# The second set of triangular inverses queued on DVE behind step 12 of the first set

## The chip, the core and the metric

The kernel runs on one core of a Trainium2 chip. The metric is the time of one execution in microseconds on the device. The core's engines each work through their own queue in order: TensorE (PE), VectorE (DVE), ScalarE (ACT) and GpSimd (POOL). SyncE (SP) issues most of the DMA transfers; ACT issues some. An instruction starts when it is at the head of its engine's queue and the semaphores it needs are set.

## The reference

One layer of a diffusion backbone: 2048 latent and 256 context tokens of width 1024 are normalised and modulated, one projection feeds two mixers (a gated DeltaNet in both directions and windowed attention), and gates, two projections and an output projection follow. Cut to the branch that matters here:

```python
qa, ka, va, g, bt = _gdn_inputs(qkv, beta_r, decay_r, conv_w, a_log, dt_bias)
oa, _, _ = _gdn_bidir(qa, ka, va, g, bt, s_f, s_b, True)
ya = _gdn_output(oa, za, gdn_norm_w)               # za: a gate, silu
...
# inside _gdn_chunked, for each chunk of 64 tokens and each head
a_mat = jnp.where(strict, jnp.einsum('nbhik,nbhjk->nbhij', kb, kc) * decay, 0.0)
t_mat = lax.linalg.triangular_solve(a_mat, eye, left_side=True, lower=True, unit_diagonal=True)
u = jnp.einsum('nbhij,nbhjv->nbhiv', t_mat, vc * bc[..., None])
```

Each chunk of 64 tokens needs the inverse of a unit lower triangular 64x64 matrix, for four heads and two directions.

## The kernel before, in words

The kernel is one program for one core. It computes in float32, with each operand of a large matmul split into a high and a low part, so that a product takes three matmuls per slice of 128 rows. A scheduler sets the order of the instructions in each engine's queue at build time, from priorities (the order in which the code is written) and its own estimate of time. `tc.issue_after(x)` adds one rule: the instructions written inside the block come after `x` in the queue of the engine on which `x` runs. It adds no wait on the chip, and it says nothing of the other engines' queues.

The stages that matter, in the order of the code:

- **Convolutions** (`qkv`, `conv`, `finish`) of q, k and v. `last_conv[0]` is the DVE instruction (L565) that ends the last one.
- **Gate products for token groups 2 and 3** (`gates`, `rest`, `rest_run`, `fm_dense`). For each of 24 column tiles (m) `rest` loads a weight tile: L241 loads `wr` on SP, ACT rounds it to `wh` (L243), DVE takes the rest as `wl` (L246). For each token group `rest_run` runs 24 matmuls (8 slices, L524 to L526) into one of three PSUM buffers `rps`. ACT takes the tanh into one of two buffers `rt` (L816). For m below 8 DVE multiplies it with the product (L818) and so is the last reader of the PSUM buffer, and SP stores the result (L819). For m from 8 on ACT's tanh is the last reader, and ACT issues the store.
- **The modulation gate** (`mod_gate`) beside them, in two halves: SP loads eight `wmg` tiles (L220), ACT scales them (L221; the first of a half goes to `gacc`), POOL adds them up (L223), and PE sums over the partitions (L227).
- **The inverses** (`base`), twice: set 0 (context chunks and the chunks that the scan meets first) and set 1 (the chunks in the middle). A set holds 128 matrices of 64x64, one per partition, in a tile `N`; set 0's lies in the pool `bs` and set 1's in `bs2`. SP loads `nb` (L733) and `N` (L734), 2 MB for a set. DVE scales `N` in four slices of rows for each direction, eight instructions (L737 and L739), and then runs 62 steps of elimination: step m multiplies a column with a row into `btmp` (L747) and adds this to the rows below m (L749), over (63 - m) x m elements per partition, so that a step grows from 62 to 992 elements and shrinks again. POOL clears the upper triangle (L754) and SP stores the set (L759).
- **The scan** (`scan`, `chain`, `merge`, `output`) over 18 chunks in both directions, with gate products for token groups 1 and 0 as filling work for PE, and a last small set of inverses (`base4`). The scan's `v` is L1102.
- Attention, the projections and the output projection follow; the change doesn't touch them.

Both sets are written behind the gate products, each inside `tc.issue_after(last_conv[0].ins)`, so that DVE may start them as soon as the convolutions are over; the scheduler mixes their steps with the drains (L818) and the `wl` (L246) of the gate products.

Of the kernel before, what the change touches and what calls it, by code (L numbers as in the profile page):

```python
# [11 lines left out]
ALU = mybir.AluOpType  # L12
# [20 lines left out]
def hybrid(tc, ins, out, dbg=None, upto=9):  # L33
    nc = tc.nc
    V, S, G, T = nc.vector, nc.scalar, nc.gpsimd, nc.tensor
    ctx = ExitStack()
    with ctx:
        _hybrid(ctx, tc, nc, V, S, G, T, ins, out, dbg, upto)


def _hybrid(ctx, tc, nc, V, S, G, T, ins, out, dbg, upto):
# [514 lines left out]
    last_conv = [None]  # L556
# [153 lines left out]
    def runs(chunks):  # L710

        out = []
        for i, c in enumerate(chunks):
            if out and c == out[-1][1] + out[-1][2]:
                out[-1][2] += 1
            else:
                out.append([i, c, 1])
        return out

    def base(si, npool, pool, fr, bk):  # L720


        n = 8 * len(fr)
        h1 = max(32, n)
        N = npool.tile([128, 64, 64], F32, name="N")
        nb = npool.tile([128, 64], F32, name="nb")
        if n < h1:
            G.memset(N[0:h1], 0.0)
            G.memset(nb[0:h1], 0.0)
        for d, chunks in ((0, fr), (1, bk)):  # L730
            for i0, c, k in runs(chunks):
                p0 = d * h1 + i0 * 8
                dma(nb[p0:p0 + 8 * k], brT[c:c + k, d * 4:d * 4 + 4].rearrange("c h (b t) -> c (h b) t", b=2))  # L733
                dma(N[p0:p0 + 8 * k], Nsp[d][c:c + k].rearrange("c h b r i -> (c h b) r i"))  # L734
        for q in range(4):
            r, w = slice(q * 16, q * 16 + 16), q * 16 + 16
            V.tensor_tensor(N[0:h1, r, 0:w], N[0:h1, r, 0:w],  # L737
                            nb[0:h1, 0:w].unsqueeze(1).to_broadcast([h1, 16, w]), op=ALU.mult)
            V.tensor_tensor(N[h1:h1 + n, r, 0:w], N[h1:h1 + n, r, 0:w],  # L739
                            nb[h1:h1 + n, r].unsqueeze(2).to_broadcast([n, 16, w]), op=ALU.mult)  # L740
        yield 9
        A = N[0:h1 + n]
        for m in range(1, 63):
            tmp = pool.tile([128, 1376], F32, name="btmp")
            r = 63 - m
            tv = tmp[0:h1 + n, :r * m].rearrange("p (r j) -> p r j", j=m)
            V.tensor_tensor(tv, A[:, m + 1:, m].unsqueeze(2).to_broadcast([h1 + n, r, m]),  # L747
                            A[:, m, 0:m].unsqueeze(1).to_broadcast([h1 + n, r, m]), op=ALU.mult)
            V.tensor_tensor(A[:, m + 1:, 0:m], A[:, m + 1:, 0:m], tv, op=ALU.add)  # L749
            yield 2 * (65 + 1.04 * r * m) / 1e3  # L750

        for q in range(4):
            r, w = slice(q * 16, q * 16 + 16), 64 - q * 16
            G.affine_select(A[:, r, q * 16:], A[:, r, q * 16:], pattern=[[1, 16], [-1, w]], base=0,  # L754
                            channel_multiplier=0, compare_op=ALU.is_gt, fill=0.0)
        V.memset(A.rearrange("p r c -> p (r c)")[:, ::65], 1.0)
        for d, chunks in ((0, fr), (1, bk)):
            p0 = d * h1
            dma(Xset[d][si].rearrange("c h b r j -> (c h b) (r j)"), N[p0:p0 + n].rearrange("p r j -> p (r j)"))  # L759
            for ci, c in enumerate(chunks):  # L760
                Xsp[d][c] = Xset[d][si][ci]
        yield 1
# [82 lines left out]
    LAST = (LAT(14, 15), LAT(0, 1))  # L845
    for si, (fr, bk, np_) in enumerate((([0, 1] + LAT(*range(0, 6)), [0, 1] + LAT(*range(10, 16)), bs),
                                        (LAT(*range(6, 14)), LAT(*range(2, 10)), bs2))):
        with tc.issue_after(last_conv[0].ins):
            for _ in base(si, np_, bs2, fr, bk):
                pass  # L850
    last_base = base4(*LAST)
# [425 lines left out]
    with tc.tile_pool(name="p4h", bufs=1, side="right", reuse_waits="tile") as hr, \  # L1277
# [15 lines left out]
        A, Y = {}, {}  # L1293
# [265 lines left out]
```

## Time and profile before

| | |
|---|---|
| time, median of 3 runs | 2011.6 us (2008.56 to 2013.08) |
| the profiled execution's own time | 2014.61 us |
| its span, first to last instruction | 2012.8 us |
| granted TensorE clock, mean | 0.983 |
| L747, 124 instructions of both sets | 659.2 to 965.3 us, 114.6 us busy |
| L749, the same | 659.5 to 966.5 us, 118.5 us busy |
| L737 and L739, scalings of both sets | 645.7 to 674.5 us |
| MATMUL L524 to L526 into `rps` | 768 each, 309.7, 309.0 and 307.8 us busy |

Times in the text are microseconds from the span's start. In a time line a row gives start, length, engine, line, operation, tiles written and read, partitions x elements, and how many instructions are merged in it; the brackets at its end give how long the engine stood before it and whose end it waited for. A matmul's length in a row holds its passage through the array, so the rate of PE is read from starts. Lines have the numbers of the kernel before, unless it is said otherwise; in the kernel after, everything from `base` on stands two lines further down (L747 is L749 there, L749 is L751, L737 is L739, L739 is L741, L818 is L820, L1102 is L1104).

### The profile page before, as it was taken

To read this page: it belongs to the slowest core of one execution; us is meant where nothing else is said; L and a number is where in the kernel's file an instruction comes from. 1 tells how busy PE (TensorE), PEld (TensorE's weight loads), DVE (VectorE), ACT (ScalarE), POOL (GpSimd) and SP (SyncE) were. 2 spreads that over 40 slices of the span, in tenths; PEclk is the share of its full clock that TensorE was granted. 3 is DMA by queue.
4 is the path that set the end of the run, shared out by engine and by line. 5 is a ranking of instruction groups with operands and counts; after the bars stand their busy time and mean duration, and the time that the engine had idled before them with its cause. 6 is when DMAs were issued, how large, how long until landed. Compare 5 with 4: busy or idle time off the path is not lost. (4 is left out here: it accounts for less than half of the span.)

```text
span 2012.8 us, 32096 instructions
## 1 busy us (share of the span) xinstructions
PE 1924.7 (96%) x10947; PEld 1611.6 (80%) x10947; DVE 1501.4 (75%) x2871; ACT 807.2 (40%) x1998; POOL 689.5 (34%) x768
## 2 busy tenths in 40 slices
PE   6999999989999999999999999999989999998998
PEld 3888888779998778877888888888778888876776
DVE  6979766667776899999777776536687768756867
ACT  5755545544443322211222233225665646532211
POOL 1652111225543211004222234323555444410675
PEclk8999999999999999999999999999999999999999
DMA  7552326764546633537887777664455545364453
GB/s 258 168 136 84 102 88 157 191 159 148 161 147 162 183 112 111 140 100 221 225 241 220 237 207 211 185 208 152 144 173 176 187 149 180 106 206 146 152 157 131
DMA packets 387703, 333.12 MB, mean 165 GB/s; under 512 B 83992, under 2 KB 307536, under 8 KB 386900
## 3 DMA queue, kind: packets, MB, share of 16 engines
q1 hardware_dynamic: 352244, 288.60, 49.7%
q10 hardware_dynamic: 35296, 42.48, 6.0%
q8 instruction: 87, 1.43, 0.3%
q14 instruction: 76, 0.62, 0.1%
HBM read 220.28 MB, written 109.13 MB: 164 GB/s over the span
## 5 line engine op out<-in xcount | busy, mean ns | idle before, releaser
L524 PE MATMUL rps<-hh,wh 128*128 128x512 f32 x768 | 309.7, 403 | 5.2 <-DVE rt L818 4.1
L526 PE MATMUL rps<-hh,wl 128*128 128x512 f32 x768 | 309.0, 403 | 0.0
L525 PE MATMUL rps<-hl,wh 128*128 128x512 f32 x768 | 307.8, 401 | 0.0
L563 DVE SCALAR_TENSOR_TENSOR cacc<-y,cw,cacc 128x512 f32<-128x512 f32 (+1 forms) x224 | 162.1, 745 | 22.6 <-ACT cacc L561 18.2
L524 PEld LDWEIGHTS rps<-hh,wh 128*128 128x128 f32 x768 | 145.7, 190 | 40.1 <-DVE rt L818 4.5
L525 PEld LDWEIGHTS rps<-hl,wh 128*128 128x128 f32 x768 | 145.9, 190 | 32.9
L524 PE MATMUL lps<-hh,wh 128*128 128x512 f32 (+1 forms) x448 | 171.4, 383 | 0.3 <-ACT y L634 0.3
L526 PEld LDWEIGHTS rps<-hh,wl 128*128 128x128 f32 x768 | 145.6, 190 | 32.5
L526 PE MATMUL lps<-hh,wl 128*128 128x512 f32 (+1 forms) x448 | 171.3, 382 | 0.0
L525 PE MATMUL lps<-hl,wh 128*128 128x512 f32 (+1 forms) x448 | 171.3, 382 | 0.0
L945 DVE TENSOR_TENSOR pl<-pt,ph 128x512 fp32r<-128x512 f32 x156 | 105.3, 685 | 42.2 <-ACT ph L943 41.6
L943 ACT CAST ph<-pt 128x512 fp32r<-128x512 f32 x156 | 90.3, 585 | 112.6 <-PE pt L941 78.0
L917 DVE CUSTOM_DVE_ANT_0 pr<-sc,band,sk 128x640 f32<-128x640 f32 (+1 forms) x128 | 106.5, 861 | 33.5 <-PE sc L913 17.5
L816 ACT ACTIVATE rt<-rps 128x512 f32<-128x512 f32 x96 | 57.2, 596 | 182.0 <-PE rps L526 168.1
L749 DVE TENSOR_TENSOR N<-N,btmp 128x62 f32<-128x62 f32 (+30 forms) x124 | 118.5, 955 | 3.0
L927 POOL TENSOR_SCALAR pr<-pr,sm 128x640 f32<-128x640 f32 (+1 forms) x128 | 99.8, 800 | 55.5 <-DVE sm L925 39.5
L747 DVE TENSOR_TENSOR btmp<-N 128x62 f32<-128x62 f32 (+30 forms) x124 | 114.6, 924 | 3.1
L919 ACT ACTIVATE pr<-pr,sm 128x640 f32<-128x640 f32 (+1 forms) x128 | 104.0, 815 | 19.8 <-DVE sm L917 19.8
L246 DVE TENSOR_TENSOR wl<-wr,wh 128x512 fp32r<-128x512 f32 x120 | 92.7, 786 | 23.9 <-POOL wh L245 20.6
L1229 PE MATMUL pps<-yh,wph 128*128 128x512 f32 x256 | 104.9, 412 | 3.9 <-DVE tb L1237 2.1
L245 POOL TENSOR_SCALAR wh<-wr 128x512 fp32r<-128x512 f32 x72 | 48.6, 690 | 169.1 <-PE lps L525 92.5
L1231 PE MATMUL pps<-yh,wpl 128*128 128x512 f32 x256 | 100.9, 395 | 0.0
(371 smaller groups left out, 5039.9 us busy)
## 6 DMA issues: line engine op xcount, KB each, us to landing
wr<-in_w_in_dram SPq DMA_DIRECT2D x120, 256.0 KB
kw<-Ksp SPq DMA_DIRECT2D x28, 384.0 KB
x<-vsp SPq DMA_DIRECT2D x36, 256.0 KB
k<-ksp SPq DMA_DIRECT2D x34, 256.0 KB
kT<-kTsp SPq DMA_DIRECT2D x34, 256.0 KB
wm<-in_w_mod_dram SPq DMA_DIRECT2D x16, 512.0 KB
xt<-in_x_dram SPq DMA_DIRECT2D x16, 512.0 KB
dtl<-Dsp SPq DMA_DIRECT2D x32, 256.0 KB
```

Of the source, the lines that this page charges most:

```text
L524: T.matmul(ps, lhsT=wh[:, k], rhs=xh[:, k], start=k == 0, stop=False)
L525: T.matmul(ps, lhsT=wh[:, k], rhs=xl[:, k], start=False, stop=False)
L526: T.matmul(ps, lhsT=wl[:, k], rhs=xh[:, k], start=False, stop=k == kt - 1)
L563: V.scalar_tensor_tensor(a, y[:, t:t + n], cw[:, m, t:t + 1], a, op0=ALU.mult, op1=ALU.add)
L747: V.tensor_tensor(tv, A[:, m + 1:, m].unsqueeze(2).to_broadcast([h1 + n, r, m]), A[:, m, 0:m].unsqueeze(1).to_broadcast([h1 + n, r, m]), o ...
L749: V.tensor_tensor(A[:, m + 1:, 0:m], A[:, m + 1:, 0:m], tv, op=ALU.add)
L917: V.tensor_tensor_reduce(s_, ps[:, o:768], band[:, b0:b0 + W + 256], -0.125, sk[:, 1, hd:hd + 1], ALU.add, ALU.min, sm[:, h, 1:2])
L919: S.activation(s_, s_, AF.Exp, scale=-1.0, bias=sm[:, h, 1:2], accum_out=sm[:, h, 2:3])
L927: G.tensor_scalar(p[:, h, :W + 256], p[:, h, :W + 256], sm[:, h, 3:4], 1.0, op0=ALU.mult, op1=ALU.mult)
L945: V.tensor_tensor(pl, pt, f32(ph), op=ALU.subtract)
L1229: T.matmul(ps, lhsT=wh[:, k, ms], rhs=hs[k], start=k == 0, stop=False)
L1231: T.matmul(ps, lhsT=wl[:, k, ms], rhs=hs[k], start=False, stop=k == 3)
```

## The change

A dictionary keeps the instruction that ends each step of each set. The second set is then written behind step 12 of the first set, and no longer behind the last convolution; the first set stays where it was.

```diff
+    step = {}
+
     def base(si, npool, pool, fr, bk):
...
-            V.tensor_tensor(A[:, m + 1:, 0:m], A[:, m + 1:, 0:m], tv, op=ALU.add)
+            step[si, m] = V.tensor_tensor(A[:, m + 1:, 0:m], A[:, m + 1:, 0:m], tv, op=ALU.add)
...
-        with tc.issue_after(last_conv[0].ins):
+        with tc.issue_after(step[0, 12].ins if si else last_conv[0].ins):
             for _ in base(si, np_, bs2, fr, bk):
                 pass
```

No instruction is added or left out, and no wait. The rule holds for DVE alone: the loads of set 1 keep their places in SP's queue. In DVE's queue the eight scalings of set 1 move. First, the queue of the kernel before, from the drain of the fourth gate product on (L818 are drains, L747 and L749 steps of set 0, L737 and L739 the scalings of set 1):

```order
L818 SCALAR_TENSOR_TENSOR rt<-rt,rps 128x512
L747 TENSOR_TENSOR btmp<-N 128x290
L737 TENSOR_TENSOR N<-N,nb 64x16x16
L737 TENSOR_TENSOR N<-N,nb 64x16x32
L737 TENSOR_TENSOR N<-N,nb 64x16x48
L737 TENSOR_TENSOR N<-N,nb 64x1024
L749 TENSOR_TENSOR N<-N,btmp 128x58x5
L739 TENSOR_TENSOR N<-N,nb 64x16x16
L739 TENSOR_TENSOR N<-N,nb 64x16x32
L739 TENSOR_TENSOR N<-N,nb 64x16x48
L739 TENSOR_TENSOR N<-N,nb 64x1024
L818 SCALAR_TENSOR_TENSOR rt<-rt,rps 128x512
```

The same place in the kernel after, from the same drain (L820) to the next:

```order
L820 SCALAR_TENSOR_TENSOR rt<-rt,rps 128x512
L749 TENSOR_TENSOR btmp<-N 128x290
L751 TENSOR_TENSOR N<-N,btmp 128x58x5
L749 TENSOR_TENSOR btmp<-N 128x342
L751 TENSOR_TENSOR N<-N,btmp 128x57x6
L749 TENSOR_TENSOR btmp<-N 128x392
L751 TENSOR_TENSOR N<-N,btmp 128x56x7
L749 TENSOR_TENSOR btmp<-N 128x440
L820 SCALAR_TENSOR_TENSOR rt<-rt,rps 128x512
```

The scalings are gone from between drains 4 and 5, and two and a half steps of set 0 stand there instead. In the kernel after they stand between drains 6 and 7, which the next rows show from drain 6 to drain 8:

```order
L820 SCALAR_TENSOR_TENSOR rt<-rt,rps 128x512
L751 TENSOR_TENSOR N<-N,btmp 128x52x11
...
L739 TENSOR_TENSOR N<-N,nb 64x16x16
L741 TENSOR_TENSOR N<-N,nb 64x16x16
...
L739 TENSOR_TENSOR N<-N,nb 64x1024
L741 TENSOR_TENSOR N<-N,nb 64x1024
L749 TENSOR_TENSOR btmp<-N 128x650
L820 SCALAR_TENSOR_TENSOR rt<-rt,rps 128x512
L246 TENSOR_TENSOR wl<-wr,wh 128x512 x2
L820 SCALAR_TENSOR_TENSOR rt<-rt,rps 128x512
```

In the kernel before, the rows between drains 6 and 7 and on to drain 8 hold steps and a pair of `wl` alone:

```order
L818 SCALAR_TENSOR_TENSOR rt<-rt,rps 128x512
L749 TENSOR_TENSOR N<-N,btmp 128x56x7
L747 TENSOR_TENSOR btmp<-N 128x440
L749 TENSOR_TENSOR N<-N,btmp 128x55x8
L747 TENSOR_TENSOR btmp<-N 128x486
L749 TENSOR_TENSOR N<-N,btmp 128x54x9
L818 SCALAR_TENSOR_TENSOR rt<-rt,rps 128x512
L747 TENSOR_TENSOR btmp<-N 128x530
...
L749 TENSOR_TENSOR N<-N,btmp 128x51x12
L246 TENSOR_TENSOR wl<-wr,wh 128x512
L818 SCALAR_TENSOR_TENSOR rt<-rt,rps 128x512
```

So the eight scalings stand in one piece behind drain 6, and drain 7 behind them, close to drain 8. The scheduler has also placed other work anew. The second half of the modulation gate comes earlier on ACT, SP and POOL: on ACT its first scaling to `gacc` stands behind the ninth tanh, where it stood behind the nineteenth. In the scan, instructions on PE and DVE change places with the fillers next to them; one place on DVE, in the kernel before (L1039 and L1102 belong to the scan, L747 and L749 to set 1):

```order
L1039 TENSOR_SCALAR gw<-gw 128x1
L749 TENSOR_TENSOR N<-N,btmp 128x12x51
L747 TENSOR_TENSOR btmp<-N 128x572
L1102 TENSOR_TENSOR v_10065<-vps,brs 128x512
L818 SCALAR_TENSOR_TENSOR rt<-rt,rps 128x512
```

and in the kernel after:

```order
L749 TENSOR_TENSOR btmp<-N 128x612
L751 TENSOR_TENSOR N<-N,btmp 128x12x51
L1104 TENSOR_TENSOR v_10065<-vps,brs 128x512
L820 SCALAR_TENSOR_TENSOR rt<-rt,rps 128x512
L749 TENSOR_TENSOR btmp<-N 128x572
```

The first `v` of the scan has moved ahead of the multiply of 572 elements.

## The prediction

> **What bounds the kernel now.** I read the busy table first, then busy time by stretches of 25 us around the instructions that the change moves, then the time lines of PE, DVE, ACT and the DMA queue there.
>
> ```profile
> PE 1924.7 (96%) x10947; PEld 1611.6 (80%) x10947; DVE 1501.4 (75%) x2871; ACT 807.2 (40%) x1998; POOL 689.5 (34%) x768
> ...
> 650.00:675.00 25.00, 21.17 (x91) 16.71 (x89) 16.77 (x28) 6.04 (x10) 3.20 (x2) 0.99 0.94 227
> 675.00:700.00 25.00, 24.76 (x94) 19.87 (x95) 24.52 (x30) 8.62 (x15) 9.71 (x8) 0.87 0.53 158
> 700.00:725.00 25.00, 25.00 (x108) 20.10 (x108) 24.66 (x29) 5.29 (x9) 0.17 (x1) 1.00 0.31 91
> ```
>
> PE is busy 96% of the span, so the end moves by what PE's stops become. The columns of a stretch are: length, then PE, PEld, DVE, ACT, POOL, the granted clock, DMA share, GB/s. From 700 PE runs 108 matmuls per 25 us; from 650 it runs 91 and from 675 it runs 94 at a clock of 0.87. PE has no other hole between 475 and 900 us, and the change moves work inside this one. From 675 DVE is full as well (24.5 of 25 us).
>
> I number the gate products as PE runs them (24 matmuls for one column tile and one token group) and call the L818 instruction that reads a product out of PSUM its drain. Three PSUM buffers rotate, so product k+3 waits for drain k. The rows show starts of products 8, 9, 10 and 11 behind the last matmul of product 7.
>
> ```profile
> 670.78 0.39 PE L526 MATMUL rps<-hh,wl 128*128 128x512 f32 x1
> 675.24 0.80 PE L524 MATMUL rps<-hh,wh 128*128 128x512 f32 x1 [4.07 <-DVE rt L818]
> ...
> 683.73 0.40 PE L524 MATMUL rps<-hh,wh 128*128 128x512 f32 x1
> ...
> 689.33 0.40 PE L524 MATMUL rps<-hh,wh 128*128 128x512 f32 x1
> ...
> 694.93 0.40 PE L524 MATMUL rps<-hh,wh 128*128 128x512 f32 x1
> ...
> 674.00:676.00 2.00, 0.76 (x2) 0.67 (x3) 1.94 (x3) 1.66 (x3) 1.92 (x2) 0.64 0.02 7
> 676.00:678.00 2.00, 2.00 (x7) 1.54 (x6) 2.00 (x2) 0.00 (x0) 1.19 (x2) 0.50 0.48 131
> 682.00:684.00 2.00, 2.00 (x11) 1.59 (x10) 1.93 (x3) 0.00 (x0) 0.66 (x1) 1.00 1.07 351
> ```
>
> PE stands 4.07 us for drain 5. Then product 8 takes 8.49 us (675.24 to 683.73) where products 9 and 10 take 5.60, because the granted clock is 0.50 until about 681. The hole costs 4.07 + 2.89 = 6.96 us.
>
> Why is drain 5 late? DVE's queue, with drains 3 to 8 at 658.56, 664.00, 674.50, 679.08, 684.45 and 692.68:
>
> ```profile
> 658.56 0.69 DVE L818 SCALAR_TENSOR_TENSOR rt<-rt,rps 128x512 f32<-128x512 f32 x1
> ...
> 664.60 0.46 DVE L747 TENSOR_TENSOR btmp<-N 128x290 f32<-128x290 f32 x1
> 665.09 3.02 DVE L737 TENSOR_TENSOR N<-N,nb 64x256 f32<-64x256 f32 x4
> 668.03 0.45 DVE L749 TENSOR_TENSOR N<-N,btmp 128x290 f32<-128x290 f32 x1
> 671.43 3.04 DVE L739 TENSOR_TENSOR N<-N,nb 64x256 f32<-64x256 f32 x4 [2.94 <-DMA N<-Nsp]
> 674.50 0.69 DVE L818 SCALAR_TENSOR_TENSOR rt<-rt,rps 128x512 f32<-128x512 f32 x1
> ...
> 678.00 0.55 DVE L747 TENSOR_TENSOR btmp<-N 128x392 f32<-128x392 f32 x1
> ...
> 679.08 0.67 DVE L818 SCALAR_TENSOR_TENSOR rt<-rt,rps 128x512 f32<-128x512 f32 x1
> ...
> 684.45 0.68 DVE L818 SCALAR_TENSOR_TENSOR rt<-rt,rps 128x512 f32<-128x512 f32 x1
> ...
> 692.68 0.68 DVE L818 SCALAR_TENSOR_TENSOR rt<-rt,rps 128x512 f32<-128x512 f32 x1
> 693.28 0.83 DVE L747 TENSOR_TENSOR btmp<-N 128x650 f32<-128x650 f32 x1
> ```
>
> L737 and L739 are the eight scalings of the second set, 3.02 + 3.04 us. They stand ahead of drain 5, and the second four wait 2.94 us for the load of N. But drain 5 has a second condition, its tanh on ACT:
>
> ```profile
> 658.19 0.49 SPq L734 DMA_DIRECT2D N<-Nsp  x1
> ...
> 659.28 0.33 SPq L819 DMA_DIRECT2D zasp<-rt  x1
> ...
> 671.71 0.60 ACT L816 ACTIVATE rt<-rps 128x512 f32<-128x512 f32 x1 [9.84 <-DMA zasp<-rt]
> ```
>
> Tanh 5 writes one of two `rt` buffers and waits until the store of drain 3, issued at 659.28 right behind the last load of N, has landed. It runs from 671.71 to 672.31, whatever DVE does.
>
> **The change part by part.**
>
> *The wait of 2.94 us that goes.* Up to 665.09 both kernels have the same queues, so load and store land as before. DVE then runs steps instead of scalings: the second half of step 5 (0.45), two of 342 elements, two of 392 (0.55 each) and one of 440, by the neighbouring sizes about 0.50 and 0.62 each: 0.45 + 1.00 + 1.10 + 0.62 and some 0.03 between instructions, 3.4 us, until 668.5. There it stands for tanh 5 until 672.31. So one wait of 2.94 us becomes another of 3.8 us; DVE's queue loses 0.9 us. Drain 5 runs from 672.31 to 673.00 instead of 674.50 to 675.19, and product 8 starts at 673.05: 2.19 us of the 4.07 are gained, 1.9 us of stop remain.
>
> *The eight scalings, 6.06 us.* They aren't saved, they are moved from before drain 5 to between drains 6 and 7. Their new place costs nothing only if product 10, which needs drain 7, can wait. The work in DVE's queue up to drain 8 is the same in both kernels, but for one multiply of 650 elements that now lies ahead (0.83 us, 0.87 with the gap). So drain 8 comes at 692.68 + 0.87 + 0.9 = 694.45. Drain 7 stands ahead of it by one drain (0.60 from start to start) and a pair of L246:
>
> ```profile
> 712.27 1.28 DVE L246 TENSOR_TENSOR wl<-wr,wh 128x512 fp32r<-128x512 f32 x2
> ```
>
> 694.45 - 1.28 - 0.60 = 692.6, so drain 7 ends at 693.3, where it ended at 685.1 before. To bound it: the additions on POOL slow DVE's steps, but not its scalings, beside which the first pair ran.
>
> ```profile
> 673.29 3.82 POOL L223 TENSOR_TENSOR gacc<-gacc,wmg 128x512 f32<-128x512 f32 x2 [11.36 <-ACT wmg L221]
> ...
> 676.00 1.47 DVE L749 TENSOR_TENSOR N<-N,btmp 128x342 f32<-128x342 f32 x1
> ```
>
> A step of about 0.50 took 1.47 beside an addition, 0.97 more; the four scalings took 3.04 beside one and 3.02 without. Now both additions at 673 fall on steps: 0 to 1.4 us more. Drain 7 ends between 693.3 and 694.7. The Trainium skill, "SBUF — State Buffer", section "SBUF: two separate sides", says that a GpSimd instruction and a VectorE instruction with two SBUF inputs exclude each other for the whole instruction; by that rule the upper end is the nearer one. The trace agrees for the step (1.47 us) and shows no such cost to the scalings, so I stay between.
>
> *What PE makes of it.* Drain 6 now has steps of 440 to 572 elements, no scalings and one L246 pair ahead of it, about 5.5 us of work after drain 5 and two or three additions beside it: it ends at 681 to 682, near 679.75 as before. Product 9 starts with it and ends near 687 to 689. Product 10 waits for drain 7 until 693.3 to 694.7, against 689.33 before: 4.0 to 5.4 us late. A new stop of 4 to 8 us takes the place of the old one, and the clock falls with it. What that costs lies between the 2.89 us above (after a stop of 4.07) and what the shortest stops nearby cost:
>
> ```profile
> 939.47 1.16 PE L1111 MATMUL sps<-v,k 128*128 128x128 f32 x8 [1.64 <-DVE v L1102]
> ...
> 940.00:945.00 5.00, 5.00 (x35) 3.85 (x33) 4.91 (x8) 0.00 (x0) 2.42 (x3) 0.66 0.67 196
> ```
>
> A stop of 1.64 us was followed by a clock of 0.66 over 5 us, 1.7 us lost. Product 11 then starts at 693.3 + 5.6 + 1.7 = 700.6 to 694.7 + 5.6 + 2.9 = 703.2, where it started at 694.93: **5.7 to 8.3 us late**, and I take 7. The Trainium skill, "TensorE: Matmul & The Clock Gate", section "HAM oscillation — how this bites in real kernels", asks for no idle gap above about 3.4 us. By that rule the stop of 1.9 us ahead of product 8 would leave the clock alone; the trace differs, 0.66 after 1.64 us. The sum is the same by both, since product 9 waits for drain 6 either way.
>
> *What follows.* From product 11 on, drains keep their places in the queue (drain 8 comes at 694.5, and product 11 ends after 706), so PE runs at full rate, 7 us late. The second half of POOL's additions now comes behind tanh 9, at about 698 to 730, and not here:
>
> ```profile
> 747.34 1.99 POOL L223 TENSOR_TENSOR gacc<-gacc,wmg 128x512 f32<-128x512 f32 x1 [3.13 <-ACT gacc L221]
> ...
> 766.03 3.47 POOL L223 TENSOR_TENSOR gacc<-gacc,wmg 128x512 f32<-128x512 f32 x2 [4.55 <-ACT wmg L221]
> ```
>
> There are seven; at 0.97 us on a step each they take 6.8 us of DVE, less than the 7 that PE is behind and what drains had in hand. DVE doesn't carry a lead over to the scan, since it waits for PE's weight buffers by then:
>
> ```profile
> 887.59 1.14 ACT L243 CAST wh<-wr 128x512 fp32r<-128x512 f32 x2 [4.76 <-PE rps L525]
> ...
> 888.24 1.29 DVE L246 TENSOR_TENSOR wl<-wr,wh 128x512 fp32r<-128x512 f32 x2 [0.85 <-ACT wh L243]
> ```
>
> At the stop of 1.64 us there is something to gain, for `v` now stands one multiply earlier:
>
> ```profile
> 938.06 0.75 DVE L747 TENSOR_TENSOR btmp<-N 128x572 f32<-128x572 f32 x1
> 938.74 0.68 DVE L1102 TENSOR_TENSOR v<-vps,brs 128x512 f32<-128x512 f32 x1
> ```
>
> 0.7 us of the stop go (938.06 to 938.74), and with them, if the rest is too short to move the clock, 1.7 more: 0.7 to 2.4, I take 1.5. The sum is 7 - 1.5 = **5.5 us more**. The profiled execution took 2014.61 us (span 2012.8) and so would take 2020.1; the median of the runs shown is 2011.6, and the forecast is made from it: 2011.6 + 5.5 = 2017.1 us.
>
> **The rivals.** *The later stops go too.* If DVE comes to the scan with a lead, the stop at 939 and a like one at 994 vanish with their clocks.
>
> ```profile
> 994.32 0.27 PE L1028 MATMUL mep<-moff,mx 64*64 64x64 f32 x1 [1.53 <-DVE moff L1025]
> ```
>
> They cost 1.64 + 1.7 and 1.53 + 1.7, 6.6 us: 7 - 6.6 gives 2012.0, no change to be seen. For it: PE is late against a queue that isn't. Against it: the rows at 888.
>
> *It does no more than move the wait* (the change not doing what it says): DVE stands for tanh 5 and not for N, drain 7 is in time, and product 8 comes 2.2 us earlier with the clock's loss cut from 2.89 to 1.7: 3.4 us less, 2008.2. This takes a drain 7 before 687, over 6 us earlier than the queue gives.
>
> *Faster, the other side.* The hole closes: 6.96 us less, 2004.6. Its price is that hole, its place product 8, and it decides at one point: the store of drain 3 must land before 668 instead of 671.7, and the queue must be through the scalings by the end of product 9. For it speaks that all of this hangs on DMA landings, which the N loads delay; against it that the same loads go out ahead of the same store.
>
> **How the numbers follow.** Under 0.2%, 4 us, a measurement of this kernel can't be told from no change. Forecast (3 to 9 us more) 60 in 100, nearly all of it slower by over 4; stops regained later, 22; the wait moved, 10; the hole closed, 8. Slower 0.57, within 0.2% 0.29, faster 0.14. The range takes in the forecast's own, 2014.6 to 2020.6 with 2 us of spread between runs (2008.56 to 2013.08 before), the second rival, and the edge of the third: 2008.2 to 2022.8.
>
> **What would show it.** Right: the wait of L739 for N is gone, tanh 5 still starts near 671.7, DVE stands before drain 5; product 8 starts near 673; drain 7 stands behind the eight scalings near 693, and PE has a stop of 4 us or more ahead of product 10 with the clock at 0.50 behind it. Wrong: no stop ahead of product 10, a store that lands early, or no stop at 939 and 994.

## The result, and the profile after

The changed kernel takes **2020.98 us** (median of 5 runs, 2019.81 to 2023.64) where the kernel before, run beside it, takes 2013.08 (5 runs, 2008.56 to 2019.57). The ratio is 1.0052 with a 95% interval of 1.0035 to 1.0069: slower, by 7.0 to 13.9 us at 2013. The forecast was 5.5 us. The profiled execution took 2019.81 us with a span of 2017.9, against 2014.61 and 2012.8 before.

The same lines as in the prediction, now of the changed kernel (its line numbers are 2 higher behind the new dictionary): the busy table, then busy time by stretches of 25 us with the granted clock, DMA share and GB/s at the end.

```profile
PE 1923.5 (95%) x10947; PEld 1609.7 (80%) x10947; DVE 1500.6 (74%) x2871; ACT 806.4 (40%) x1998; POOL 690.7 (34%) x768
```

```profile
650.00:675.00 25.00, 24.53 (x105) 19.44 (x105) 17.19 (x28) 6.86 (x11) 4.54 (x3) 1.00 0.94 240
675.00:700.00 25.00, 18.04 (x56) 12.97 (x55) 24.67 (x28) 6.82 (x11) 8.36 (x6) 0.80 0.47 144
700.00:725.00 25.00, 25.00 (x109) 20.11 (x108) 24.66 (x23) 9.00 (x15) 12.80 (x7) 1.00 0.44 130
```

The hole has moved from 650 to 675 into 675 to 700 and has grown: PE stands 0.47 + 6.96 us in these two stretches (3.83 + 0.24 before), and at a granted clock of 0.80 its 18.04 busy us lose about another 3.6, if the half clock is taken as spread evenly over the stretch (0.87 and 3.2 before). The time line of PE shows the stops:

```profile
671.44 0.50 PE L524 MATMUL rps<-hh,wh 128*128 128x512 f32 x1 [0.47 <-DVE rt L820]
681.41 0.79 PE L524 MATMUL rps<-hh,wh 128*128 128x512 f32 x1 [4.11 <-DVE rt L820]
689.99 1.02 PE L227 MATMUL gsum<-gacc,mats 128*1 128x512 f32 x2
693.76 0.58 PE L524 MATMUL rps<-hh,wh 128*128 128x512 f32 x1 [2.76 <-DVE rt L820]
```

One stop of 4.07 us became three, ahead of products 8, 9 and 10: 0.47 + 4.11 + 2.76 = 7.34. By the starts of the products the half clock costs more than that mean says: product 9 takes 8.58 us (681.41 to the `gsum` pair at 689.99) and product 10 takes 7.26, where 5.60 is the full rate, so 4.6 us are lost (2.89 before). Product 11 starts at 701.02 (694.93 before). Two matmuls of `gsum`, 1.02 us, now run inside the hole; before, they came later. Behind the stops stand ACT's tanh 5 and DVE's queue, with POOL beside it:

```profile
670.06 0.60 ACT L818 ACTIVATE rt<-rps 128x512 f32<-128x512 f32 x1 [8.85 <-DMA zasp<-rt]
...
670.69 0.69 DVE L820 SCALAR_TENSOR_TENSOR rt<-rt,rps 128x512 f32<-128x512 f32 x1 [2.54 <-ACT rt L818]
...
671.94 1.65 DVE L749 TENSOR_TENSOR btmp<-N 128x486 f32<-128x486 f32 x1
673.62 1.64 DVE L751 TENSOR_TENSOR N<-N,btmp 128x486 f32<-128x486 f32 x1
...
677.27 1.82 DVE L749 TENSOR_TENSOR btmp<-N 128x572 f32<-128x572 f32 x1
679.02 1.74 DVE L246 TENSOR_TENSOR wl<-wr,wh 128x512 fp32r<-128x512 f32 x1
680.68 0.68 DVE L820 SCALAR_TENSOR_TENSOR rt<-rt,rps 128x512 f32<-128x512 f32 x1
...
686.82 1.96 DVE L741 TENSOR_TENSOR N<-N,nb 64x768 f32<-64x768 f32 x1
688.79 2.22 DVE L739 TENSOR_TENSOR N<-N,nb 64x1024 f32<-64x1024 f32 x1
691.02 1.22 DVE L741 TENSOR_TENSOR N<-N,nb 64x1024 f32<-64x1024 f32 x1
...
693.03 0.68 DVE L820 SCALAR_TENSOR_TENSOR rt<-rt,rps 128x512 f32<-128x512 f32 x1
...
671.54 3.20 POOL L223 TENSOR_TENSOR gacc<-gacc,wmg 128x512 f32<-128x512 f32 x2 [10.36 <-ACT wmg L221]
676.72 3.49 POOL L223 TENSOR_TENSOR gacc<-gacc,wmg 128x512 f32<-128x512 f32 x2 [1.98 <-ACT wmg L221]
686.35 3.59 POOL L223 TENSOR_TENSOR gacc<-gacc,wmg 128x512 f32<-128x512 f32 x2 [6.13 <-ACT wmg L221]
```

The wait of DVE for N (2.94) is gone; it waits 2.54 for tanh 5 instead, which waits for the store of drain 3, as forecast. Each of POOL's six additions to `gacc` lengthens one DVE instruction by about 1 us, scalings and L246 too: of the two scalings of 64x1024 one takes 1.22, the other 2.22.

In the scan the second of the two stops named in the prediction, 1.53 us at 994.32, has grown. The changed kernel's time line of PE, of DVE (the last step of the second set, and the scalings just ahead of `moff`), and of the DMA queue:

```profile
944.32 1.16 PE L1113 MATMUL sps<-v,k 128*128 128x128 f32 x8 [1.55 <-DVE v L1104]
...
1001.28 0.36 PE L1030 MATMUL mep<-moff,mx 64*64 64x64 f32 x1 [3.84 <-DVE moff L1027]
...
973.31 0.21 DVE L751 TENSOR_TENSOR N<-N,btmp 128x62 f32<-128x62 f32 x1
...
997.03 3.86 DVE L786 TENSOR_TENSOR N<-N,btmp 32x256 f32<-32x256 f32 x4 [7.09 <-DMA N<-Nsp]
...
975.00 1.16 SPq L761 DMA_DIRECT2D Xsp<-N  x2
...
988.28 0.79 SPq L779 DMA_DIRECT2D N<-Nsp  x2
```

The same DVE and DMA queue rows of the kernel before:

```profile
966.46 0.21 DVE L749 TENSOR_TENSOR N<-N,btmp 128x62 f32<-128x62 f32 x1
966.59 1.11 DVE L1117 SCALAR_TENSOR_TENSOR S<-S,tot,sps 128x128 f32<-128x128 f32 x4
...
989.23 4.71 DVE L784 TENSOR_TENSOR N<-N,btmp 32x256 f32<-32x256 f32 x4 [3.25 <-DMA N<-Nsp]
...
968.56 1.15 SPq L759 DMA_DIRECT2D Xsp<-N  x2
...
981.15 0.88 SPq L777 DMA_DIRECT2D N<-Nsp  x2
```

`moff` stands in DVE's queue behind the scalings of the last inverses, and these wait for an N that is loaded only when the second set has been stored (`Xsp<-N`). That store went out 33.5 us after the scan's first matmul before (935.05) and 35.0 after it now (939.99). The last step of the second set stood ahead of the scan's second update of `S` (966.59) and of a `moff` before; now it stands behind both, at 973.31.

### The profile page after: what moved, and what is told of

Read it like the earlier page. It is cut to its first block, busy times and chain, and to the rows that moved or that the text cites. A ratio compares the mean times of both kernels' runs of the same rounds, so it can differ in the third digit from the quotient of the medians.

```text
span 2017.9 us, 32092 instructions
## 1 busy us (share of the span) xinstructions
PE 1923.5 (95%) x10947; PEld 1609.7 (80%) x10947; DVE 1500.6 (74%) x2871; ACT 806.4 (40%) x1998; POOL 690.7 (34%) x768
## 5 line engine op out<-in xcount | busy, mean ns | idle before, releaser
L818 ACT ACTIVATE rt<-rps 128x512 f32<-128x512 f32 x96 | 57.3, 597 | 187.4 <-PE rps L526 165.2
L749 DVE TENSOR_TENSOR btmp<-N 128x62 f32<-128x62 f32 (+30 forms) x124 | 117.3, 946 | 3.0
L246 DVE TENSOR_TENSOR wl<-wr,wh 128x512 fp32r<-128x512 f32 x120 | 91.0, 774 | 27.9 <-POOL wh L245 19.6
L1232 PE MATMUL pps<-yl,wph 128*128 128x512 f32 x256 | 101.1, 396 | 0.0
```

The costliest lines, as they stand in the source:

```text
L1232: T.matmul(ps, lhsT=wh[:, k, ms], rhs=ls[k], start=False, stop=False)
```

## The experiments

To compare traces I cut each at two places that all kernels have: from the first gate product's first matmul (628.39 before, 628.19 after) to the scan's first `vps` matmul, "**ahead of the scan**", and from there to the last `ksps` matmul, "**scan**". PE has the same work in each part in all of them but e2 and e3, so differences are stops and lost clock. "1000" is PE's stop of the last rows above. Ratios are to runs of the kernel before on the same chip.

| run | ratio, 95% interval | ahead of the scan | scan | 1000 |
|---|---|---|---|---|
| before, and twice again (e8, e16) | | 306.7, 306.5, 308.0 | 371.8, 367.8, 371.2 | 1.53, 1.72, 1.90 |
| changed, and twice again (e1, e14) | 1.0054 (1.0039 to 1.0070) | 311.8, 312.8, 313.8 | 371.5, 370.6, 371.6 | 3.84, 3.88, 3.99 |
| e2 step 8 | 1.0123 (1.0103 to 1.0143) | 314.1 | 386.7 | |
| e3 step 31 | 1.0083 (1.0068 to 1.0099) | 308.2 | 391.5 | |
| e4 late loads, and twice again (e13, e15) | 1.0010 (0.9996 to 1.0024) | 306.5, 306.5, 306.3 | 371.2, 374.3, 372.9 | 3.97, 4.46, 3.06 |
| e5 changed, small additions | 1.0038 (1.0024 to 1.0051) | 305.4 | 373.7 | 4.90 |
| e6 changed, loads behind the store | 1.0063 (1.0047 to 1.0079) | 312.0 | 371.1 | 3.79 |
| e7 paced additions | 0.9994 (0.9982 to 1.0007) | 308.7 | 365.2 | 1.61 |
| e9 paced, spread loads | 0.9999 (0.9986 to 1.0012) | 306.4 | 366.3 | 1.41 |
| e10 before, spread loads | 1.0020 (1.0007 to 1.0032) | 308.4 | 369.0 | 1.69 |
| e11 before, small additions | 1.0003 (0.9990 to 1.0016) | 304.2 | 373.1 | 2.03 |
| e12 changed, spread loads | 1.0004 (0.9990 to 1.0018) | 304.9 | 367.0 | 1.55 |

One property of the runs is not in the table: the order of PE's instructions in the scan, which the scheduler makes. It is one order (I call it the first) in before, e7, e9, e10, e11 and e12, row for row; another (the second) in the changed kernel, e4, e5 and e6, which by the traces differs from the first at some 46 places and about 380 of PE's 10947 rows, between 941 and 1143 us; and e2 and e3 have orders of their own, over 2000 rows away from the first. DVE's order in the scan goes with PE's: some 95 of its rows differ between the first and the second.

**The changed kernel again (e1).** No edit.

> The changed kernel once more, with a second profile. First theory (the hole between products 7 and 11 sets the difference): product 11 again starts 5.5 to 6.5 us later than in the kernel before, measured from the start of product 7, and the median is 5 to 8 us above it. Rival (the later stops of the scan decide, and they vary from execution to execution): the hole is the same, but the stops and clock dips between 939 and 1280 us come out otherwise than in the first profile of this kernel (1.55 us without a dip, 3.84 us with a dip, 2.03 us without a dip), and the difference of the medians lies outside 5 to 8 us.

2017.79 us against 2006.63. Product 11 is 7.3 us later than before, measured from the same start (of this 1.7 is `gsum`). The later stops were 1.37, 3.88 and 3.74: the middle one is no accident of one execution. The difference, 11 us, lies outside 5 to 8.

**The scalings put elsewhere (e2, e3).**

```diff
-        with tc.issue_after(step[0, 12].ins if si else last_conv[0].ins):
+        with tc.issue_after(step[0, 8].ins if si else last_conv[0].ins):     (e2)
+        with tc.issue_after(step[0, 31].ins if si else last_conv[0].ins):    (e3)
```

> The second set is queued behind step 8 instead of step 12: all eight scalings then stand between drains 5 and 6, with the loads as in the changed kernel. First theory (scalings ahead of drain 7 cost product 10's wait): drain 6 ends near 681 as in the changed kernel, drain 7 follows within 2 us instead of 12, the stop ahead of product 9 stays at about 4 us, the stop of 2.76 us ahead of product 10 is gone, product 11 starts 2.8 to 5 us earlier than in the changed kernel, and the time is 3 to 5 us below it. Rival (PE is late because of POOL's additions and tanh 5 alone): product 11 starts within 1 us of the changed kernel.

> The second set is queued behind step 31: its scalings stand behind drain 16, past the hole, with the loads as in the changed kernel. First theory: stop ahead of product 9 as in the changed kernel (about 4 us, because tanh 5 and POOL's additions are as they were), none ahead of product 10, product 11 2.8 to 5 us earlier than in the changed kernel, time 3 to 5 us below it. Rival (the scan's stops near 994 to 1001 hang on when the second set's N is freed): that stop grows beyond 3.84 us, since the second set ends later, and takes the gain back: no change against the changed kernel.

In the time lines of PE and DVE of e2 stand:

```profile
689.61 0.79 PE L524 MATMUL rps<-hh,wh 128*128 128x512 f32 x1 [9.92 <-DVE rt L820]
...
681.50 2.19 DVE L739 TENSOR_TENSOR N<-N,nb 64x1024 f32<-64x1024 f32 x1
...
685.53 3.43 DVE L246 TENSOR_TENSOR wl<-wr,wh 128x512 fp32r<-128x512 f32 x2
688.88 0.67 DVE L820 SCALAR_TENSOR_TENSOR rt<-rt,rps 128x512 f32<-128x512 f32 x1
```

e2 missed: with scalings, a pair of L246 (3.43 instead of 1.28) and all of the additions in front of drain 6, that drain came at 688.88 and PE stood 9.92 us. e3 met its expectation for the stops of the hole (4.12 ahead of product 9, none ahead of product 10): 308.2 ahead of the scan, 4.6 less than the mean of the changed kernel (312.8). Its time is still 16.7 us above before, since its scan takes 391.5 us. That is not the stop at 1000 (0.59 in its trace) but the scan's new order, with waits of up to 3.08 us for loads in other places; the rival had the right sign for another reason. So e2 and e3 say nothing of the change by their times, only by their holes.

**Loads behind drain 9 (e4).** As e3, and

```diff
+        with tc.issue_after(stored[8].ins) if si else nullcontext():
             for d, chunks in ((0, fr), (1, bk)):
...
-        (dma if m < 8 else adma)(dst[gi][mm], t)
+        stored.append((dma if m < 8 else adma)(dst[gi][mm], t))
```

> As behind step 31, and the second set's loads of nb and N issued behind the store of drain 9 instead of ahead of that of drain 3. First theory (tanh 5 waits because the store of drain 3 stands behind 2 MB of loads): that store lands within 4 us of its issue, tanh 5 runs near 665 to 667, drain 5 no longer waits, the stops ahead of products 8, 9 and 10 fall from 7.3 us together to under 2, no stretch at half clock lies between 665 and 700, product 11 starts 6 to 7 us earlier than in the kernel before and 11 to 13 earlier than in the changed kernel; the time is 5 to 7 us below the kernel before. Rival (DVE's queue with POOL's additions is too full whatever lands): drain 6 stays near 680 and a stop of 3 us or more stays ahead of product 9; time within 3 us of the kernel before.

The time lines of ACT, PE and POOL:

```profile
664.81 0.58 ACT L819 ACTIVATE rt<-rps 128x512 f32<-128x512 f32 x1
...
680.85 0.80 PE L524 MATMUL rps<-hh,wh 128*128 128x512 f32 x1 [4.34 <-DVE rt L821]
...
670.36 3.15 POOL L223 TENSOR_TENSOR gacc<-gacc,wmg 128x512 f32<-128x512 f32 x2 [2.88 <-ACT wmg L221]
675.40 1.29 POOL L223 TENSOR_TENSOR gacc<-gacc,wmg 128x512 f32<-128x512 f32 x1 [1.89 <-ACT wmg L221]
677.54 1.45 POOL L223 TENSOR_TENSOR gacc<-gacc,wmg 128x512 f32<-128x512 f32 x1 [0.84 <-ACT wmg L221]
```

Both were half right. Tanh 5 ran at 664.81 without a wait, and there is no stop ahead of product 8. But drain 6 stayed at 680, behind steps that four additions stretched, and PE stood 4.34 us there. The hole has the size that it had before (306.5 ahead of the scan), at another place. With the second scan order this kernel is 2 us slower than before by its medians, and the interval (0.9996 to 1.0024) takes in no change.

**POOL's additions taken away (e5, e11).** The same edit in the changed kernel and in the one before; both leave out the modulation gate's sum but for 8 of 512 columns:

```diff
-                    G.tensor_tensor(gacc, gacc, wm, op=ALU.add)
+                    G.tensor_tensor(gacc[:, 0:8], gacc[:, 0:8], wm[:, 0:8], op=ALU.add)
```

> The changed kernel with POOL's additions to gacc cut to 8 of 512 columns (the modulation gate's sum is left out but for those columns); nothing else differs, and PE's order is the same row for row. Theory now (POOL's additions hold up DVE's steps, scalings and L246 by about 1 us each, so drains 6 and 7 are late): the steps of 486 and 572 elements take 0.67 and 0.75 us instead of 1.65 and 1.82, the eight scalings 6.1 instead of 8.4; drain 6 ends near 677, the stop of 4.11 us ahead of product 9 falls below 1, a stop of 3 to 5 us stays ahead of product 10 (the scalings still stand there); idle time and lost clock between 655 and 740, 11.4 and 12.4 us in the two profiles of the changed kernel, fall to 7 to 9, the time by 3 to 5 us. Rival (tanh 5's wait sets it): stop ahead of product 9 stays at 3 us or more and the time within 2 us of the changed kernel.

> The kernel before with POOL's additions to gacc cut to 8 of 512 columns (the modulation gate's sum is left out but for those columns); PE's order is the same row for row. Theory: the hole of the kernel before hangs on loads (N at 671.4, the store of drain 3 at 671.7), not on additions: stop and half clock ahead of product 8 stay at 4 to 5 and 2 to 3 us, against 11.9 falling to 5.7 in the changed kernel by the same edit; the stops of the scan are as before; time within 2 us of the kernel before. Rival (the additions hold DVE up in both): the loss between 655 and 740 falls below 4 us, time 3 us or more below.

The time lines of PE and DVE of e5:

```profile
671.17 0.50 PE L524 MATMUL rps<-hh,wh 128*128 128x512 f32 x1 [1.81 <-DVE rt L820]
687.31 0.51 PE L524 MATMUL rps<-hh,wh 128*128 128x512 f32 x1 [2.18 <-DVE rt L820]
...
671.68 0.67 DVE L749 TENSOR_TENSOR btmp<-N 128x486 f32<-128x486 f32 x1
...
683.34 1.22 DVE L739 TENSOR_TENSOR N<-N,nb 64x1024 f32<-64x1024 f32 x1
```

And that of PE of e11:

```profile
676.07 0.80 PE L524 MATMUL rps<-hh,wh 128*128 128x512 f32 x1 [3.07 <-DVE rt L818]
```

In e5 the steps, the scalings and L246 have their undisturbed lengths up to drain 8, the stop ahead of product 9 is gone (2.18 us stay ahead of product 10, where 3 to 5 were expected), and the part ahead of the scan is 7.4 us shorter than in the changed kernel (305.4 against 312.8). In the kernel before the same edit saves 2.9 (304.2 against 307.1), more than the theory allowed, less than the rival asked. Without the additions the change would cost 1.2 us ahead of the scan (one trace of each, and traces of one kernel differ by up to 2 us there); with them it costs 5.7. By the ratios e5 gains only 3 us on the changed kernel and e11 nothing on the kernel before; both traces have a scan at the long end (373.7, 373.1). What the change costs falls by 3.8 us by the ratios (0.54% to 0.38 - 0.03%) and by 4.5 by the traces.

**Loads behind drain 3's store instead of ahead of it (e6).** The changed kernel with `stored[2]` where e4 has `stored[8]`.

> The changed kernel with the second set's loads of nb and N issued right behind the store of drain 3 instead of right ahead of it; PE's order is the same row for row. Rival theory (DVE's wait for tanh 5, 2.5 us, pushes drains 6 and 7): tanh 5 runs before 668, DVE's wait ahead of drain 5 is gone, drains 6 and 7 come 2.5 us earlier, the stops ahead of products 9 and 10 shrink by as much, the time falls by 2 to 3 us. Theory now (additions and scalings set it): the additions move onto the steps instead, drain 6 stays within 1 us of 681, and the idle time and lost clock between 655 and 740 stay within 1.5 us of 11.4 to 12.4.

ACT's time line:

```profile
671.49 0.72 ACT L221 ACTIVATE wmg<-wmg,silc 128x512 f32<-128x512 f32 x1 [5.41 <-DMA wmg<-in_w_mod_dram]
672.12 0.58 ACT L819 ACTIVATE rt<-rps 128x512 f32<-128x512 f32 x1
```

Neither side's premise came about. Tanh 5 no longer waited for the store, but it stood in ACT's queue behind a product with `wmg`, whose load had now been issued between the two loads of N. ACT took that load up 7.1 us after its issue at 664.37. The hole is unchanged (312.0). So whether DVE's wait for tanh 5 pushes drains 6 and 7 stays untested.

**Additions one at a time, then also loads in pieces (e7, e9).** e7 is e4 with each load of `wmg` queued behind the store of the product before it. e9 cuts the second set's N into eight loads, each behind a store of its own:

```diff
-                dma(wm, ins["w_mod"][0, k * 128:(k + 1) * 128, cs_])
+                with tc.issue_after(stored[-1].ins):
+                    dma(wm, ins["w_mod"][0, k * 128:(k + 1) * 128, cs_])
...
+                with tc.issue_after(stored[6 + 1 * (2 * part + d)].ins) if si else nullcontext():
...
-                dma(N[p0:p0 + 8 * k], Nsp[d][c:c + k].rearrange("c h b r i -> (c h b) r i"))
+                dma(N[p0:p0 + 8 * k, rs], Nsp[d][c:c + k, :, :, rs].rearrange("c h b r i -> (c h b) r i"))
```

> As the run with late loads (second set behind step 31, its loads behind the store of drain 9), and each load of wmg issued behind the store of the product before it, so that POOL's additions come one to a column tile instead of six within 15 us; PE's order is that of the kernel before, row for row. Theory now: with neither scalings nor bunched additions ahead of drains 5 to 7 there is no stop above 1 us and no half clock between 655 and 740, where the kernel before loses 7.0 us; the stops at 939 and 994 are as in the kernel before; the time is 5 to 7 us below the kernel before. Rival (what is won here is given back in the scan, where DVE still has the same work to end): the hole is gone but the stops between 900 and 1300 grow by as much, and the time stays within 2 us of the kernel before.

> As the paced run, but the second set's 2 MB of N come in eight loads of 256 KB, one behind each of the stores of drains 7 to 14. In the paced run ACT stood 12.64 us for a load of wmg that had been issued just ahead of 2 MB of N, and PE then 3.18 us. Theory (a burst of 2 MB holds up whatever load or store heads an in-order queue): that stop at 713 and its half clock go, what is left is the 1.5 us ahead of product 11; idle time and lost clock between 655 and 740 fall from 7.4 us to 1 to 3, and with PE's order that of the kernel before the time is 4 to 6 us below the kernel before. Rival (DVE has too much work here, and the stop only moves once more): 6 us or more are lost again in this stretch, and the time is within 2 us of the kernel before.

The time lines of ACT and PE of e7:

```profile
708.77 0.72 ACT L224 ACTIVATE wmg<-wmg,silc 128x512 f32<-128x512 f32 x1 [12.64 <-DMA wmg<-in_w_mod_dram]
...
713.75 0.80 PE L527 MATMUL rps<-hh,wh 128*128 128x512 f32 x1 [3.18 <-DVE rt L824]
```

And that of PE of e9:

```profile
689.75 0.51 PE L527 MATMUL rps<-hh,wh 128*128 128x512 f32 x1 [1.54 <-DVE rt L827]
...
774.70 0.50 PE L529 MATMUL rps<-hh,wl 128*128 128x512 f32 x1 [2.01 <-DVE wl L249]
```

In e7 the hole ahead of products 8 to 10 is gone, and a new one stands at 713, where ACT stood 12.64 us for `wmg`. The expectation of e9 misreads this wait: the load that ended it was issued at 702.19, 9 us behind the 2 MB and not ahead of them, and ACT took it up 6.6 us later, where it took up the loads before and after it within 2.9 (690.51 to 693.39, 716.93 to 719.72). ACT stood 8.2 to 9.1 us for `wmg` at the neighbouring column tiles too, because the load is queued behind a store, so the 2 MB account for about 4 us of the 12.64. In e9 the new hole is gone too. Up to 730 its PE is more than 3.5 us ahead of the kernel before, but this lead melts until 775, where PE waits for DVE's `wl`; ahead of the scan it has 306.4 against 306.5 to 308.0. From 655 to 775 DVE is busy 94% of the time in e9 and 96% in the kernel before. I take from this that the hole of the kernel before is mostly the place where a full DVE shows; that is argued, not shown. Neither kernel is faster; both theories expected 4 to 7 us.

**Loads in pieces alone (e10, e12).** The eight loads in the kernel before (e10) and, behind the stores of drains 2 to 9, in the changed kernel (e12).

> The kernel before with only this edit: the second set's N comes in eight loads of 256 KB behind the stores of drains 7 to 14; the additions stay bunched, and PE's order is the same row for row. Theory: tanh 5 and drain 5 are in time, no stop ahead of product 8; but five additions fall on DVE's steps between drains 5 and 6, so a stop of about 4 us stands ahead of product 9, as in the run with late loads, with half a clock behind it: 6 to 7.5 us lost between 655 and 740, time within 2 us of the kernel before. Rival (the burst of loads is the whole cause): less than 3 us lost, time 4 to 6 us below.

> The changed kernel (second set behind step 12) with the second set's N in eight loads of 256 KB behind the stores of drains 2 to 9, by which its scalings spread over drains 6 to 10, and PE's order in the scan becomes that of the kernel before, row for row. Theory (the stop of 3.8 to 4.9 us near 1000 belongs to the scan's order and not to when the second set starts): that stop is 1.5 to 1.8 us as in the kernel before; 6 to 9 us are lost between 655 and 740; time 0 to 3 us above the kernel before. Rival (a second set queued behind step 12 ends later, which delays the next N): the stop is 3 us or more.

The time line of PE of e12:

```profile
678.87 0.50 PE L524 MATMUL rps<-hh,wh 128*128 128x512 f32 x1 [1.92 <-DVE rt L826]
686.73 0.50 PE L524 MATMUL rps<-hh,wh 128*128 128x512 f32 x1 [1.99 <-DVE rt L826]
...
990.96 0.27 PE L1036 MATMUL mep<-moff,mx 64*64 64x64 f32 x1 [1.55 <-DVE moff L1033]
```

e10 as the theory had it for the hole (4.19 us ahead of product 9, then half clock), and 3.6 us slower by its medians, where the theory allowed 2. e12 settles the stop at 1000: the second set is queued behind step 12, as in the changed kernel, but the scan has the first order, and the stop is 1.55. It belongs to the scan's order. With scalings spread over five drains nothing above 2 us is left of the hole: 4.2 us of stops and no half clock between 655 and 740, less than the 6 to 9 expected.

**Repeats (e8, e13 to e16).**

> The kernel before once more, for a second profile. If the hole is a matter of queue order, stop and clock dip ahead of product 8 come again at 4.1 and 2.9 us (each within 0.5). If the stops of the scan vary from execution to execution, the idle time and lost clock between 920 and 1300, 14.6 us in the first profile, come out 2 us or more otherwise.

> The late-loads kernel once more, for a second profile. If its first profile was an execution with more stops than usual, the scan (first to last matmul of the state's chain, 371.2 us in the first profile) comes out at 367 to 370 here and the part before the scan again at 306.5 within 0.5. If the hole of the changed kernel also costs later, the scan is 371 again here.

> The changed kernel once more, third profile: 311.8 to 312.8 us from the first column-tile product to the scan in the first two, 370.6 and 371.5 in the scan. If executions differ in the scan only, the first figure stays within 0.5 us of these and the second spreads by 2 us or more; if the hole itself varies, the first one does.

> The late-loads kernel, third profile: as for the second one.

> The kernel before, third profile: 306.5 to 306.7 us before the scan and 371.8 and 367.8 in it so far. If the spread of the medians lies in the scan, the first figure repeats within 0.5 us and the second falls between 365 and 373.

Ahead of the scan each kernel repeats within 2 us (e14, at 313.8, and e16, at 308.0, lie outside the 0.5 expected); the scan of the kernel before spreads by 4, that of the changed kernel by 1. So of e14's two readings the second holds: in the changed kernel it is the hole that varies. The hole of the kernel before varies too: in e8 the stop was 4.77 and its half clock cost 2.08 us, neither within the 0.5 expected. The second profile of the kernel before took 2007.55 us, the third 2016.45. The late-loads kernel's scan came out longer again (374.3, 372.9), so its first trace was not an unlucky one; these two executions took 2020.09 and 2017.40 us, above all twelve of e4 (2003.40 to 2014.31), and beside them the changed kernel took 2019.81 and the kernel before 2016.45 and 2010.24.

## Why the prediction was right in sign and half the size

**Right.** The wait for N became a wait for tanh 5, which waits for a store behind 2 MB of loads. Drain 7 came at 693.03 behind the eight scalings (forecast: ending 693.3 to 694.7), product 10 stood for it, product 11 started at 701.02 (700.6 to 703.2), and the clock fell with the stops.

**Right by errors that cancel.** I had one stop of about 1.9 us ahead of product 8 and one of 4 to 8 us ahead of product 10. The store landed earlier than before, against my word that it would land as before (tanh 5 at 670.06, not 671.71), so product 8 lost 0.47 us and no clock (1.03 and 1.34 in the other two traces). The main stop then came ahead of product 9, which waits for drain 6. That wait followed from my own times and I didn't name it: product 8 would have ended at 678.7 and drain 6 at 681 to 682.

That drain 7 came within my bounds is in part luck: the 1.65 us that tanh 5 gained were used up again. The eight scalings took 6.65 us without additions (e5: 679.14 to 685.79) and not 6.06. And the additions cost DVE 6.1 us: 1.0 each on two steps of 486, one of 572, a scaling of 64x768, one of 64x1024 and, by the undisturbed rows of e5, L246 (1.74 against 0.71). In the kernel before they had cost 4.9 between drains 5 and 8, by its steps of 342 to 572 elements against those of e11. So 1.2 us came on top, within the 0 to 1.4 that I allowed, though the upper end was given there without its working. What I had wrong was the reading that the additions leave the scalings alone (3.04 us beside an addition). In that row it was POOL that had waited: two additions took 3.82 us. The Trainium skill, "SBUF — State Buffer", section "SBUF: two separate sides", has the two engines exclude each other for a whole instruction; the trace agrees (2.22 against 1.22 for the same scaling), and I should have gone by it.

**The term of 7 us.** Product 11 came 6.3 and 7.3 us late in the first two traces, but 1.0 to 1.7 of this is the `gsum` pair, which is moved and not lost. I had not looked at that row. Ahead of the scan the change costs 312.8 - 307.1 = **5.7 us** (means of three traces each). Of these, 4.5 go with the additions (e5 and e11: 7.4 - 2.9).

**The step that failed is "What follows".** I took 1.5 us off for the stop at 939 and left the stop at 994 as it was. The first did not shrink (1.55, 1.37 and 1.50 after, 1.64, 1.32 and 1.24 before): `v` stands one multiply earlier in the queue, but DVE stood about one instruction further back, and `v` came 3.59 us after the scan's first matmul (943.58), where it had come 3.69 after (938.74). The half clock behind that stop, which I wanted to save, was only in the first of the three traces of the kernel before. The second stop grew to 3.8 to 4.0. I had followed the moved instructions inside the hole and not the scan's order, which the scheduler makes anew 250 us later. Over all traces the scan takes 368.9 us with the first order (8 traces, 365.2 to 373.1) and 372.1 with the second (8 traces, 370.6 to 374.3): **3.2 us more, where I had 1.5 less** (in the three traces each of the kernel before and the changed kernel alone 1.0 more). e12 and e4 show that the stop at 1000 goes with the order: 1.55 with step 12 and the first order, 3.97 with step 31 and the second. The rows of DVE show the way: in all eight traces with the second order the last step of the second set stands behind the second update of `S` and `moff` (1.11 + 0.41 us), in the eight with the first order ahead of them; and its store goes out 34.8 to 35.7 us after the scan's first matmul, instead of 31.9 to 33.5, so the N of the last inverses is loaded later.

5.7 + 3.2 = 8.9 us lies within the measured 7.0 to 13.9. **Open:** the three traces of each kernel differ by only 5.6 us in span (2016.7 against 2011.1 on average): 5.7 ahead of the scan, 1.0 in it and about 1.3 less behind it. Two of the three traced executions of the kernel before had long scans. By the medians of runs taken side by side the changed kernel and e4 are 9 us apart where their traces show 6.4 ahead of the scan and 1.6 the other way in it; and e5 is by its ratio 7.6 us slower than the kernel before, where its trace shows 1.7 less ahead of the scan and 4.8 more in it than the first order's mean. Executions of one kernel differ by up to 13 us, and most have no trace. Of the 2.6 us by which the second order stores the second set later, the update of `S` and `moff` explain 1.5; the rest was not taken apart.

## What to carry to other kernels

Where an engine is full for a hundred microseconds, moving its work about inside that stretch moves the stop, not the end: five arrangements of loads, scalings and additions (e4, e7, e9, e10, e12) came out within 0.2% of the kernel before by their medians, none measurably ahead of it, while the one under study cost 0.5%. Ask of each moved piece which other engine's work it will now lie beside, and read a shared cost from the row of the engine that waited. And where a scheduler makes the order, compare the whole order, far behind the edit as well: an edit of one number cost 16.7 us (e3) in a part of the program that it didn't name, while its own place had become better.

## What the runs showed of the hardware

- DVE instructions with two SBUF operands and POOL's additions hold each other up, whichever came first: 2.22 instead of 1.22 us for a scaling, 3.43 instead of 1.28 for a pair of L246, and 3.82 instead of about 2.6 for two additions.
- What is issued just behind 2 MB of loads lands late: a store of 256 KB (tanh 5 waited 8.85 us for it), or a load of 256 KB (taken up 7.1 us after its issue in e6 and 6.6 in e7, 2.9 in e7 with no 2 MB ahead of it). An in-order engine then holds up all behind it.
- Stops of 4 us were always followed by half clock here. Of stops of 1.3 to 2 us some were and some were not: in the kernel before 1.64 us at 939 cost 1.7 us in one trace, 1.32 nothing in the next; at 994 both cost 1.7; in e7 1.61 us there cost nothing.
- Much of that is where the stop falls. Between 640 and 1320 us half clock stands in each trace only in whole pieces of 3.41 us on one grid: in the kernel before two pieces from 674.58, one from 940.82 and one from 995.43, 78 and 94 pieces after the first. Over all traces a piece there at full clock in which PE stood 1.95 us or more was always followed by a piece at 0.50, one with less than 1.48 never, and in between both happened. The 1.64 us lie whole in one piece (937.40 to 940.82, PE busy 1.78); the 1.92 and 1.99 us of e12 are split between two (1.62 and 1.33 in the larger part) and cost no clock.
